# Moving two loads to later places in the block, and turning the inner order of a spreading copy

## Chip, cores and metric

The kernel runs on one core of one Trainium2 chip. The metric is device time in microseconds; the time before is the median of three runs.

## What is computed

```python
batch, n_heads, seq, head_dim = 8, 12, 1024, 64
# q, k: float32, (8, 12, 1024, 64)
out = np.einsum('bhid,bhjd->bhij', q, k)   # float32, (8, 12, 1024, 1024)
```

These are attention scores for 96 heads, without scaling or softmax. The inputs are 50.33 MB, the output is 402.65 MB.

## The kernel before

**Blocks, parts, pairs.** The first 8 heads are done by the class `First` in a start phase. The other 88 heads form 11 blocks ("units") of 8 heads. A block has two `Part`s (number 2u and 2u + 1), and a part has two passes `g` = 0 and 1. One pass computes two heads at once and is called a pair here; so a block has four pairs, and the 22 parts have 44.

**Loads.** `load(2u, ...)` brings Q of block u, `load(2u + 1, ...)` brings K, each 2048 KB, into a tile x_sb of `in_pool`, which has two buffers. A load can therefore be issued only when the tile of the block before last has been read by all its casts. ACT's queue issues these loads.

**Casts on POOL.** `Part.cast` turns a part's Q and K from float32 into float16 and stacks the heads on the partitions. It fills four `half_sb` tiles (Q in two pieces, then K in two), each by four casts of 32 partitions. `half_pool` has four buffers, so a cast into a tile waits until DVE has transposed what the tile held, a part earlier.

**Transposes on DVE (L208, L212).** `Part.transpose(x, c)` turns one half tile. For K it goes through `step_sb` and a copy that puts the elements in order.

**Spaced weights on DVE (L222).** `Part.space(g)` writes the turned Q of two heads into a tile that is zero otherwise (`spaced_even` for g = 0, `spaced_odd` for g = 1): head s = 0 lies on partitions 0 to 63 in the even columns, head s = 1 on partitions 64 to 127 in the odd columns. It is two copies of 64 partitions x 1024 elements. A 128 x 128 slice of the tile is then the weights of a product that yields 64 rows of each of the two heads.

**Products and copies (L75, L76).** `Part.scores(g, side)` makes 16 products of 128 x 1024 for a pair, each of two matmuls into a PSUM tile (four tiles), and copies each to the output tile `o_sb`: copies 1, 4, 7, 10 and 13 (counted from 0) by DVE, the others by ACT. Then SP issues one DMA of 8192 KB for the pair (L238). `out_pool` has two buffers, so a pair's first copies wait until the output of the pair before last has landed.

**The order is written by hand.** `pin` keeps each engine's instructions in program order. The dictionary `side` says what is emitted behind which copy. Behind copy 13 of g = 0 stand `space(1)` of the same part and three of the next part's four transposes; behind copy 13 of g = 1 stand the fourth transpose, `transpose(1, 1)`, and `space(0)` of the next part. Before the change the loads stood at these places: in the last pair of a block (odd part, g = 1) Q of the block after next behind copy 2 and K behind copy 12, both on ACT's queue. The casts of part n + 3 were emitted behind part n.

Of the kernel before, what the change touches and what calls it, by code (L numbers as in the profile page):

```python
# [13 lines left out]
def kernel(  # L14
# [6 lines left out]
    nc = tc.nc  # L21

    B, H, S, D = q.shape
    NT = S // P
# [19 lines left out]
    spaced = [spaced_even, spaced_odd]  # L44
# [46 lines left out]
    class First:  # L91
# [7 lines left out]
        def load(self):  # L99
            m = S * D // P  # L100
            for n in range(self.N if self.N == 2 else 1):
                for x in range(2):
                    start = (self.first + n) * S
                    count = S if self.N == 2 else self.N * S
                    src = (qf, kf)[x][start : start + count]
                    width = count * D // P
                    pin(
                        (nc.sync, nc.scalar)[x].dma_start(
                            out=self.raw[x][:, n * m : n * m + width],
                            in_=src.rearrange("(p r) d -> p (r d)", p=P),  # L110
                        )
                    )
# [66 lines left out]
    class Part:  # L179
# [35 lines left out]
                )  # L215

        def space(self, g):
            sp = spaced[g].rearrange("c t (i a) s -> c a t i s", a=4)
            for s in range(2):
                cs = slice(s * D, (s + 1) * D)  # L220
                qT = self.turned[0][cs].rearrange("c (a t g i) -> c g a t i", a=4, t=2 * NT, g=2)
                pin(nc.vector.tensor_copy(out=sp[cs, :, :, :, s], in_=qT[:, g]))  # L222

        def scores(self, g, side):
# [48 lines left out]
    def do_for(number, name, *args):  # L273
        if number < len(parts):
            getattr(parts[number], name)(*args)
# [18 lines left out]
    for n in range(4):  # L294
        side = {1: [lambda n=n: do_for(0, "transpose", *divmod(n, 2))]}
# [5 lines left out]
    for number, part in enumerate(parts):  # L301
        for g in range(2):
            side = {13: []}
            if g:
                side[13].append(lambda: do_for(number + 1, "transpose", 1, 1))
                side[13].append(lambda: do_for(number + 1, "space", 0))
            else:
                side[13].append(lambda: part.space(1))
                for x, c in ((0, 0), (0, 1), (1, 0)):
                    side[13].append(lambda x=x, c=c: do_for(number + 1, "transpose", x, c))  # L310
            if number == g == 0:
                side[2] = [lambda: load(3, nc.scalar)]
            if number % 2 and g:
                unit = number // 2
                side[2] = [lambda: load(2 * (unit + 2), nc.scalar)]
                side[12] = [lambda: load(2 * (unit + 2) + 1, nc.scalar)]
            part.scores(g, side)
        if number == 0:
            do_for(2, "cast")
        do_for(number + 3, "cast")  # L320


# [28 lines left out]
```

## Time and profile before

| | |
|---|---|
| median of three runs | 1082.76 us (1079.37 to 1083.43) |
| profiled execution, time | 1080.31 us |
| profiled execution, span | 1078.5 us |
| granted TensorE clock, mean | 0.72 |
| DVE, PE, ACT, POOL busy | 65%, 50%, 47%, 47% |
| DMA traffic | 420 GB/s over the span |

The engines are PE (matmul), PEld (its weight loads), DVE, ACT, POOL and SP; a q behind the name means the engine's sequencer, which issues DMAs. A row of a group of instructions reads: line, engine, operation, output <- input, shapes, count | busy us, mean ns | idle time ahead of them and what ended it. A row of the timeline begins with the start and the duration in us; brackets hold the idle time before it and what ended that. A row of a window gives the length, each engine's busy time (number of instructions), the granted TensorE clock, the DMA engines' busy share and GB/s. A row of a DMA queue gives packets, MB and the share of the time of all 16 DMA engines.

### The profile page before, as it was taken

What the parts mean: (1) busy time and instruction counts of PE and PEld (TensorE: products, weight loads), DVE (VectorE), ACT (ScalarE), POOL (GpSimd) and SP (SyncE); (2) the same over time, 40 slices, a digit from 0 to 9 for tenths busy, and PEclk for the clock granted to TensorE, in tenths of its full rate; (3) what the DMA queues carried; (4) which work ended last, traced back from release to release, by engine and by line L of the source; (5) the groups of instructions that cost most, each with busy time, mean ns of one, the idle gap of its engine ahead of it and who ended that gap; (6) DMA issues with size and microseconds to landing.
All of it is one profiled execution on the core that took longest, in us unless ns stands there. A gap on an engine that the chain in (4) does not pass through costs nothing.

```text
span 1078.5 us, 4965 instructions
## 1 busy us (share of the span) xinstructions
PE 542.9 (50%) x1568; PEld 188.9 (18%) x1568; DVE 706.4 (65%) x451; ACT 511.6 (47%) x546; POOL 510.4 (47%) x384
## 2 busy tenths in 40 slices
PE   6963454455454445444545454544454545464550
PEld 3321121111111111111111111211111111121210
DVE  3835667675677667768567765776856776578640
ACT  5963454344453445534446344553444634464550
POOL 6971743646437354354643636435464363643000
PEclk9997667676686766767678666876667866687775
DMA  9999999999999999999899999999999999999998
GB/s 378 430 430 430 443 430 414 429 428 380 439 428 427 390 429 432 394 448 430 370 444 436 420 400 426 428 391 434 445 377 448 436 420 399 426 430 428 443 442 360
DMA packets 12122, 453.30 MB, mean 420 GB/s; under 512 B 1344, under 2 KB 1344, under 8 KB 2368
## 3 DMA queue, kind: packets, MB, share of 16 engines
q1 hardware_dynamic: 8352, 406.85, 87.3%
q10 hardware_dynamic: 3744, 46.14, 11.3%
q8 instruction: 12, 0.20, 0.1%
q14 instruction: 14, 0.11, 0.0%
HBM read 50.33 MB, written 402.65 MB: 420 GB/s over the span
## 4 chain that ended last, share of the span: by engine, by line
DMA 48%; PE 17%; DVE 14%; ACT 10%; POOL 5%; issue 2%; ACTq 0%; SPq 0%; DVEq 0%
DMA out_dram<-o_sb 42%; PE ps L75 17%; ACT o_sb L76 10%; DVE spaced_even L222 6%; POOL half_sb L85 5%; DMA out_dram<-early 3%; DMA out_dram<-singles 2%; DVE o_sb L76 2%; DVE spaced_odd L222 2%; DVE step_sb L208 2%; DVE kT L212 1%; DVE qT L208 0%; DMA early<-in_q_dram 0%; PE ps L131 0%; ACT singles L76 0%
## 5 line engine op out<-in xcount | busy, mean ns | idle before, releaser
L85 POOL CAST half_sb<-x_sb 32x1024 f16<-32x1024 f32 x352 | 484.9, 1378 | 460.7 <-DVE qT L208 338.0
L76 ACT COPY o_sb<-ps 128x1024 f32<-128x1024 f32 x484 | 453.5, 1041 | 519.0 <-DMA out_dram<-o_sb 326.6
L76 DVE COPY o_sb<-ps 128x1024 f32<-128x1024 f32 x220 | 269.4, 1224 | 317.1 <-PE ps L75 197.4
L75 PE MATMUL ps<-kT,spaced_odd 128*128 128x512 f16 x704 | 257.1, 530 | 265.8 <-ACT o_sb L76 135.6
L75 PE MATMUL ps<-kT,spaced_even 128*128 128x512 f16 x704 | 225.9, 476 | 224.2 <-DVE spaced_even L222 185.9
L75 PEld LDWEIGHTS <-spaced_odd 128*128 128x128 f16 x704 | 87.2, 127 | 435.7 <-issue 293.4
L75 PEld LDWEIGHTS <-spaced_even 128*128 128x128 f16 x704 | 79.8, 116 | 370.5 <-DVE spaced_even L222 196.2
L222 DVE COPY spaced_even<-qT 64x1024 f16<-64x1024 f16 x44 | 140.2, 3187 | 0.3
L222 DVE COPY spaced_odd<-qT 64x1024 f16<-64x1024 f16 x44 | 107.0, 2431 | 1.0
L212 DVE COPY kT<-step_sb 128x1024 f16<-128x1024 f16 x44 | 62.5, 1420 | 1.6
L75 PE MATMUL ps<-kT,qT 64*128 64x512 f16 x128 | 56.0, 613 | 9.0 <-ACT early L76 6.3
L208 DVE STREAM_TRANSPOSE step_sb<-half_sb 128x1024 f16<-128x1024 f16 x44 | 53.7, 1220 | 3.9 <-POOL half_sb L85 3.9
L208 DVE STREAM_TRANSPOSE qT<-half_sb 128x1024 f16<-128x1024 f16 x44 | 52.3, 1227 | 0.7
L76 ACT COPY early<-ps 128x1024 f32<-128x1024 f32 x32 | 30.0, 1150 | 8.5 <-POOL half_sb L85 6.3
L76 ACT COPY singles<-ps 128x1024 f32<-128x1024 f32 x28 | 26.5, 1190 | 4.2 <-PE ps L75 4.2
L75 PEld LDWEIGHTS <-qT 64*128 64x128 f16 x128 | 18.7, 154 | 44.4 <-issue 42.1
L85 POOL CAST half_sb<-early 32x1024 f16<-32x1024 f32 x16 | 16.5, 1033 | 4.4 <-DMA early<-in_q_dram 3.7
L143 DVE STREAM_TRANSPOSE kT<-half_sb 128x1024 f16<-128x1024 f16 x2 | 9.8, 4908 | 0.0
L143 DVE STREAM_TRANSPOSE qT<-half_sb 128x1024 f16<-128x1024 f16 x2 | 9.6, 4793 | 0.0
L133 DVE COPY qT<-ps 128x1024 f16<-128x1024 f16 x2 | 2.4, 1224 | 9.6 <-PE ps L131 9.6
L76 DVE COPY singles<-ps 128x1024 f32<-128x1024 f32 x4 | 4.9, 1224 | 4.3 <-PE ps L75 4.3
L131 PE MATMUL ps<-ident,half_sb 128*128 128x128 f16 x32 | 4.1, 310 | 5.9 <-POOL half_sb L120 5.8
(13 smaller groups left out, 15.8 us busy)
## 6 DMA issues: line engine op xcount, KB each, us to landing
x_sb<-in_k_dram ACTq DMA_DIRECT2D x11, 2048.0 KB, 13.3
x_sb<-in_q_dram ACTq DMA_DIRECT2D x10, 2048.0 KB, 19.4
out_dram<-singles SPq DMA_DIRECT2D x4, 4096.0 KB, 22.9
out_dram<-early SPq DMA_DIRECT2D x4, 4096.0 KB, 26.3
x_sb<-in_q_dram SPq DMA_DIRECT2D x1, 2048.0 KB, 19.6
early<-in_k_dram ACTq DMA_DIRECT2D x4, 256.0 KB, 5.5
early<-in_q_dram SPq DMA_DIRECT2D x4, 256.0 KB, 5.0
early<-in_q_dram SPq DMA_DIRECT2D x1, 1024.0 KB, 10.3
```

The lines of the kernel that those rows point to most:

```text
L75: pin(nc.tensor.matmul(ps[:, at], weights, kT[:, at]))
L76: pin(copy(out=dst, in_=ps))
L85: nc.gpsimd.tensor_copy(out=half_sb[to : to + QUAD].rearrange("p (r d) -> p r d", d=32), in_=raw[b : b + QUAD, rows, h],)
L131: pin(nc.tensor.transpose(t_ps[:, t], self.halves[x][:, t], ident))
L133: pin(copy(out=dst, in_=t_ps.rearrange("c t m -> c m t")))
L143: nc.vector.transpose(out=dst.rearrange("c (i r) -> c r i", i=QUAD), in_=self.halves[x, part].rearrange("p (r i) -> p r i", i=QUAD),)
L208: pin(nc.vector.transpose(out=dst.rearrange("c (r i) -> c r i", i=QUAD), in_=src))
L212: nc.vector.tensor_copy(out=kT[:, c], in_=step_sb.rearrange("c (r i) -> c i r", i=QUAD))
L222: pin(nc.vector.tensor_copy(out=sp[cs, :, :, :, s], in_=qT[:, g]))
```

## The change

The access patterns of `space` are turned: the innermost dimension of both sides is now `a` (4 elements: 4 bytes apart in the spaced tile, 1024 bytes apart in the turned Q) where it was `i` (16 elements: 16 bytes apart in the spaced tile, side by side in the turned Q). The same elements go to the same places.

The load of Q is emitted behind copy 14 (the 15th) of the block's last pair, and that of K behind copy 8 (the 9th) of the next block's first pair. The casts of the two parts that come next but one are emitted together behind each even part, so that they stand behind both loads.

```diff
         def space(self, g):
-            sp = spaced[g].rearrange("c t (i a) s -> c a t i s", a=4)
+            sp = spaced[g].rearrange("c t (i a) s -> c t i a s", a=4)
             for s in range(2):
                 cs = slice(s * D, (s + 1) * D)
-                qT = self.turned[0][cs].rearrange("c (a t g i) -> c g a t i", a=4, t=2 * NT, g=2)
+                qT = self.turned[0][cs].rearrange("c (a t g i) -> c g t i a", a=4, t=2 * NT, g=2)
                 pin(nc.vector.tensor_copy(out=sp[cs, :, :, :, s], in_=qT[:, g]))
...
-            if number == g == 0:
-                side[2] = [lambda: load(3, nc.scalar)]
-            if number % 2 and g:
-                unit = number // 2
-                side[2] = [lambda: load(2 * (unit + 2), nc.scalar)]
-                side[12] = [lambda: load(2 * (unit + 2) + 1, nc.scalar)]
+            if number % 2 == g:
+                side[14 if g else 8] = [lambda: load(number + 3, nc.scalar)]
             part.scores(g, side)
-        if number == 0:
-            do_for(2, "cast")
-        do_for(number + 3, "cast")
+        if number % 2 == 0:
+            do_for(number + 2, "cast")
+            do_for(number + 3, "cast")
```

## Prediction

> **What bounds the kernel now.** I read the page first (span, traffic, the chain of waits), then the list of waits, then the windows, then the timeline of one block engine by engine.
>
> ```profile
> span 1078.5 us, 4965 instructions
> PE 542.9 (50%) x1568; PEld 188.9 (18%) x1568; DVE 706.4 (65%) x451; ACT 511.6 (47%) x546; POOL 510.4 (47%) x384
> HBM read 50.33 MB, written 402.65 MB: 420 GB/s over the span
> DMA 48%; PE 17%; DVE 14%; ACT 10%; POOL 5%; issue 2%; ACTq 0%; SPq 0%; DVEq 0%
> ```
>
> No engine is busy over 65%, and DMA is the largest part of the chain that ended last. The question is whether the DMA engines are ever short of work. Three windows answer it; the last two columns are the DMA share and GB/s.
>
> ```profile
> 160.00:970.00 810.00, 399.53 (x1162) 138.06 (x1160) 559.46 (x362) 373.34 (x399) 400.74 (x288) 0.70 0.99 420
> 970.00:1065.00 95.00, 42.69 (x128) 14.92 (x128) 54.52 (x37) 43.44 (x47) 10.02 (x5) 0.69 1.00 431
> 531.00:541.00 10.00, 7.19 (x20) 2.59 (x21) 4.45 (x4) 6.37 (x7) 3.18 (x2) 0.58 0.82 287
> ```
>
> In the last block, which has no loads, the traffic runs at 431 GB/s; in the nine blocks with loads at 420; and inside one of those there are 10 us at 287. So the DMA engines are the limit nearly always, and there is a hole once a block. The list of waits names what makes the hole (total us, times, longest):
>
> ```profile
> ACT o_sb L76 <- DMA out_dram<-o_sb: 326.6, 30, 15.5
> ...
> ACT o_sb L76 <- POOL half_sb L85: 127.2, 17, 11.4
> ```
>
> The 326.6 us are harmless: ACT waits for an output buffer, so DMA is behind. The 127.2 us are not: nothing in ACT's copies reads half_sb. What does wait for POOL are the loads that ACT issues, because their x_sb tile is free only after POOL's casts. ACT's timeline around the block change at 511 us:
>
> ```profile
> 511.27 1.93 ACT L76 COPY o_sb<-ps 128x1024 f32<-128x1024 f32 x2 [8.68 <-DMA out_dram<-o_sb]
> 516.40 0.33 ACTq L177 DMA_DIRECT2D x_sb<-in_q_dram  x1
> 516.78 6.51 ACT L76 COPY o_sb<-ps 128x1024 f32<-128x1024 f32 x7 [3.59 <-POOL half_sb L85]
> 534.26 0.34 ACTq L177 DMA_DIRECT2D x_sb<-in_k_dram  x1
> 534.63 12.10 ACT L76 COPY o_sb<-ps 128x1024 f32<-128x1024 f32 x13 [11.34 <-POOL half_sb L85]
> 562.12 4.89 ACT L76 COPY o_sb<-ps 128x1024 f32<-128x1024 f32 x5 [15.38 <-DMA out_dram<-o_sb]
> ...
> 582.41 10.18 ACT L76 COPY o_sb<-ps 128x1024 f32<-128x1024 f32 x11 [9.60 <-DMA out_dram<-o_sb]
> 601.71 1.93 ACT L76 COPY o_sb<-ps 128x1024 f32<-128x1024 f32 x2 [9.12 <-DMA out_dram<-o_sb]
> ```
>
> The pair that starts at 511.27 is the last of its block. Its Q load stops ACT for 3.59 us and its K load for 11.34 us, because the K load needs a cast that needs a transpose which stands behind the 14th copy of this very pair. POOL and DVE show that loop, and SP shows its price:
>
> ```profile
> 507.08 13.62 POOL L85 CAST half_sb<-x_sb 32x1024 f16<-32x1024 f32 x12 [15.28 <-DVE qT L208]
> 524.89 9.33 POOL L85 CAST half_sb<-x_sb 32x1024 f16<-32x1024 f32 x4 [4.19 <-DVE step_sb L208]
> ```
>
> ```profile
> 523.59 1.23 DVE L208 STREAM_TRANSPOSE step_sb<-half_sb 128x1024 f16<-128x1024 f16 x1
> ...
> 525.79 6.46 DVE L222 COPY spaced_even<-qT 64x1024 f16<-64x1024 f16 x2
> ```
>
> ```profile
> 536.59 0.54 SPq L238 DMA_DIRECT2D out_dram<-o_sb  x1
> ```
>
> Transpose at 523.59, casts until 534.22 (four take 9.33 us beside the spaced copies of 525.79, where twelve took 13.62), K load at 534.26, last ACT copies, output issued at 536.59. That is 25.3 us after the pair got its buffer at 511.27, where an undisturbed pair takes 10.2 us (ACT's row at 582.41: 10.18). Over 25 us after the last landing the output before it must have left, and SP's queue is empty: this is the hole of the 287 GB/s row.
>
> **How big the hole is.** An output is 128 x 16 x 1024 x 4 bytes, 8192 KB. Between the buffer waits that end at 582.41 and 601.71 one output passes with no load beside it: 19.30 us. A load is 8 heads x 1024 x 64 x 4 bytes, 2048 KB, a quarter. The Q load issued at 606.39, alone:
>
> ```profile
> 606.39 0.33 ACTq L177 DMA_DIRECT2D x_sb<-in_q_dram  x1
> ```
>
> ```profile
> DMA to landing us min/median/max: 19.4/19.4/19.4
> ```
>
> It lands at 625.8. From 582.4 to 625.8 two outputs and this load pass, 2.25 outputs in 43.4 us, and 2.25 x 19.30 is 43.4: a load between queued outputs costs its bytes and no more. A block (four outputs, Q, K) is 4.5 x 19.30 = 86.9 us of full DMA. Measured:
>
> ```profile
> 221.70 2.84 ACT L76 COPY o_sb<-ps 128x1024 f32<-128x1024 f32 x3 [8.96 <-PE ps L75]
> ```
>
> ```profile
> 942.07 2.84 ACT L76 COPY o_sb<-ps 128x1024 f32<-128x1024 f32 x3 [9.10 <-DMA out_dram<-o_sb]
> ```
>
> These are the same point of the block, eight blocks apart: 720.4 / 8 = 90.05 us. The hole is 3.2 us a block, nine times (the loads of the third to the eleventh block are issued at this place): 28.8 us at most. The other bound prices a load by its queue's row of the whole page:
>
> ```profile
> q1 hardware_dynamic: 8352, 406.85, 87.3%
> q10 hardware_dynamic: 3744, 46.14, 11.3%
> ```
>
> That is 2.31 us of all engines per MB of q1 (nearly all outputs) and 2.64 for q10 (loads), so the two loads of a block, 4.19 MB, would take 1.4 us more and the hole would be 1.8 us. I hold to 3.2, because the 43.4 us are a stretch in which DMA had no gap, and q10's row contains the gaps.
>
> **The change, part by part.**
>
> Q load, from behind copy 3 to behind copy 15 of the last pair. It needs the first 8 of the 12 casts at 507.08, over at 516.4. Copy 15 of an undisturbed pair is done some 9.2 us after the buffer, at about 520.5: no wait, 4 us to spare. The 3.59 us stall goes. Behind it on ACT stands one copy; the issue costs 0.33 us, as before.
>
> K load, from behind copy 13 of that pair to behind copy 9 of the next block's first pair. With no stall the 14th copy is over near 520.4, the transpose follows, and the four casts end by 531 even at their present 9.33 us. The next pair gets its buffer when the output in flight has landed, near 533, and its ninth copy is some 6 us later, 539: no wait, 8 us to spare. The 11.34 us stall goes, and the output now issued at 536.59 goes out near 522, while the one before it is still in flight for over 10 us. The hole is closed from both sides.
>
> What comes later: the loads land later, and share the engines with outputs all the time. How fast is a load then? While both queues had work (520 to 531 us; packets, MB, share):
>
> ```profile
> q1 hardware_dynamic: 57, 3.21, 67.4%
> q10 hardware_dynamic: 70, 1.15, 24.3%
> ```
>
> 1.15 MB of load in 11 us, so 2.10 MB take 20 us. Q: issued 520.5, landed near 543, where the first pair's transposes (behind its copy 14, near 542) let POOL start on it: level, at most a few us late. K follows on the same queue and lands near 563. It is first needed for the transpose behind copy 14 of the block's third pair: that pair gets its buffer two outputs and a load after 533, near 579, and reaches copy 14 near 588. The four casts between take up to 9.3 us: 16 us to spare. SP's queue holds only outputs and is not touched. The casts are written out later, but POOL's order of parts is the same: nothing. In the first block the K load goes from behind copy 3 to behind copy 9, once, and its data is used a pair later: nothing.
>
> The spaced copies (L222). Before, 16 elements are read side by side and written 16 bytes apart; now four are read 1024 bytes apart and written 4 bytes apart. The rows of this copy and its neighbours:
>
> ```profile
> L222 DVE COPY spaced_even<-qT 64x1024 f16<-64x1024 f16 x44 | 140.2, 3187 | 0.3
> L222 DVE COPY spaced_odd<-qT 64x1024 f16<-64x1024 f16 x44 | 107.0, 2431 | 1.0
> L212 DVE COPY kT<-step_sb 128x1024 f16<-128x1024 f16 x44 | 62.5, 1420 | 1.6
> ...
> L143 DVE STREAM_TRANSPOSE kT<-half_sb 128x1024 f16<-128x1024 f16 x2 | 9.8, 4908 | 0.0
> ```
>
> L212 reads 64 bytes apart and writes densely: 1.42 us. L143 writes 64 bytes apart: 4.91 us. So far-apart writes are dear and far-apart reads cheap. I bound the new copy by 1.4 and 4.9 us and take 1.4, the row with the like reads, no row having reads as far apart as 1024 bytes. It saves 8 x (2.81 - 1.4) = 11 us of DVE per block, and I count it at nothing: what hides it is the wait for output buffers. If that cover were gone, it would be a gain.
>
> The Trainium skill (SBUF — State Buffer, the note on cachelines under Door 1: The DMA port swizzle) says that an SBUF line has 16 bytes, that full rate needs two or more hits on a line, and that every access to a new line pays. By it the writes come right (four on a line) and the reads go wrong (each on a new line), which is the rule behind rival C below. The L212 row, with such reads at 1.42 us, bears it out only in small part, and C has its chance by that.
>
> **Sum.** 28.8 us is the whole hole. I take 2.9 of the 3.2 us per block, leaving 0.3 for handovers between outputs: 26 us. Span 1078.5 - 26 = 1052.5; the profiled execution took 1080.31, 1.8 more than its span, so 1054.3; that execution was 2.45 under the median of 1082.76, so 1056.5 for a median.
>
> **Rivals.**
>
> *A: part of the hole stays.* The loads land 20 us after they start, and Q is only level with its first use. If POOL's casts slip far enough that one pair in four still sends its output late, half the gain stays away: 1082.8 - 13 = 1069.8. For it: Q's landing. Against: what waits for POOL comes a pair and a half later.
>
> *B: no change.* Loads beside queued outputs would cost more than their bytes, and what ACT gains the DMA loses: 1082. The 43.4 us against 43.4 above speak against it; only for K's part there is no such row.
>
> *C: slower, by the far reads.* DVE's chain per pair is not far under DMA's time:
>
> ```profile
> 545.00 4.87 DVE L222 COPY spaced_odd<-qT 64x1024 f16<-64x1024 f16 x2
> ...
> 562.14 1.22 DVE L76 COPY o_sb<-ps 128x1024 f32<-128x1024 f32 x1 [6.87 <-DMA out_dram<-o_sb]
> ...
> 570.97 1.23 DVE L208 STREAM_TRANSPOSE step_sb<-half_sb 128x1024 f16<-128x1024 f16 x1
> ...
> 590.85 4.88 DVE L222 COPY spaced_odd<-qT 64x1024 f16<-64x1024 f16 x2
> ```
>
> ```profile
> 579.69 3.59 PE L75 MATMUL ps<-kT,spaced_even 128*128 128x512 f16 x8 [8.98 <-DVE spaced_even L222]
> ```
>
> From 545.00 to 570.97, less the 6.87 us wait, are 19.1 us; from 570.97 to 590.85, less some 2.0 us (a first product from 579.69 is ready near 580.4, its buffer at 582.41), 17.9. Twice both is 74 us a block, with eight spaced copies of 2.81 us mean in it, 22.5. DVE reaches the 86.9 us when a copy takes (86.9 - 74 + 22.5) / 8 = 4.4 us, and the 90.05 us at 4.8. At L143's 4.9 us a block is 90.7; nine blocks are 6 us worse than now, and the last one, now 4 x 19.30 = 77.2, becomes 90.7, 13 more: about 1102. It decides from 4.8 us per copy on, twice the undisturbed row.
>
> **How the numbers follow.** About 0.5% (5.4 us) is what a measurement of this kernel can tell from no change. Forecast 0.78, rival A 0.09, rival B 0.05, rival C 0.08. Faster takes the forecast and A: 0.87; same 0.05; slower 0.08. The forecast's own range is 1051 (28.8 us off, and the 2.45 us not added: 1051.5) to 1066 (the hole of 1.8 us, nine times, off 1082.76: 1066.6); reaching to A I give 1051 to 1070.
>
> **What would show it.** Right: ACT's wait for POOL's half_sb in the loop near 0 from 127.2; loads issued without a wait; windows of loaded blocks at 430 GB/s; same points of the block 87 us apart; landing of Q near 20 us; the L222 rows at 1 to 2 us with no effect of their own. Wrong: a block still at 90 us with 430 GB/s absent; DVE or PE waiting for POOL casts; L222 above 4.4 us, with ACT no longer waiting for out_dram.

## The result and the profile after

The changed kernel takes 1077.19 us in the median of 20 runs (1072.29 to 1081.84), the kernel before 1082.36 in 20 runs beside it (1079.37 to 1083.55). The runs after scatter more than those before. The ratio is 0.9953, with a 95% interval of 0.9939 to 0.9967; ratios here and below leave out one execution, the longest of run 9, which is marked as slow. The forecast was 1056.5, the range 1051 to 1070: the sign came, and a fifth of the size (5.2 us of 26). The profiled execution after took 1076.11 us, with a span of 1074.3.

The page after, in its parts on engines, DMA queues and the chain of waits:

```profile
span 1074.3 us, 4965 instructions
PE 540.6 (50%) x1568; PEld 190.6 (18%) x1568; DVE 579.9 (54%) x451; ACT 515.3 (48%) x546; POOL 429.4 (40%) x384
...
q1 hardware_dynamic: 8352, 406.85, 88.4%
q10 hardware_dynamic: 3744, 46.14, 10.5%
...
DMA 69%; ACT 13%; PE 8%; POOL 4%; issue 2%; ACTq 0%; POOLq 0%
```

DMA's part of the chain rose from 48 to 69%, and DVE, which had 14%, is gone from it. The engines no longer hold the DMA up, and yet the traffic of the loaded blocks is short of the 430 GB/s that was expected of them (the first row is nine blocks with loads, the second the last block; the last two columns are DMA share and GB/s):

```profile
160.00:970.00 810.00, 393.32 (x1152) 138.15 (x1152) 454.62 (x364) 375.95 (x398) 331.32 (x290) 0.70 1.00 424
970.00:1065.00 95.00, 43.51 (x128) 15.33 (x128) 40.61 (x34) 41.36 (x44) 3.85 (x3) 0.68 1.00 430
```

The share is 1.00 where it was 0.99, and still a block with loads moves only 424 GB/s: the DMA engines are busy, and not at their best. The two queue rows say the same for the whole span. (A packet is the piece of a transfer that one DMA engine moves at a time; here 64 KB of an output, 16 KB of a load.) Before, the packets of both queues took 98.6% of 1078.5 us, 1063 us, and 15 us were left; after, they take 98.9% of 1074.3, again 1062 us, with 12 left. So the change removed some 3 us of idle time and made the same bytes hardly cheaper. Within this sum it did move time: q10, nearly all of it loads, falls from 11.3% of 1078.5 to 10.5% of 1074.3, 9 us less, and q1, the outputs, rises from 87.3% to 88.4%, 8 us more. The loads became cheaper, and the outputs dearer by almost as much.

ACT's timeline at the place that the prediction read (the four pairs of one block and the first of the next):

```profile
508.00 4.89 ACT L76 COPY o_sb<-ps 128x1024 f32<-128x1024 f32 x5 [8.29 <-DMA out_dram<-o_sb]
...
516.84 0.33 ACTq L177 DMA_DIRECT2D x_sb<-in_q_dram  x1
...
530.95 5.81 ACT L76 COPY o_sb<-ps 128x1024 f32<-128x1024 f32 x6 [11.84 <-DMA out_dram<-o_sb]
535.80 0.33 ACTq L177 DMA_DIRECT2D x_sb<-in_k_dram  x1
...
557.12 4.89 ACT L76 COPY o_sb<-ps 128x1024 f32<-128x1024 f32 x5 [14.78 <-DMA out_dram<-o_sb]
...
579.53 4.89 ACT L76 COPY o_sb<-ps 128x1024 f32<-128x1024 f32 x5 [11.47 <-DMA out_dram<-o_sb]
...
598.84 8.73 ACT L76 COPY o_sb<-ps 128x1024 f32<-128x1024 f32 x9 [8.18 <-DMA out_dram<-o_sb]
```

SP's timeline at the same place:

```profile
519.14 0.54 SPq L238 DMA_DIRECT2D out_dram<-o_sb  x1
```

The stalls of 3.59 and 11.34 us are gone: both loads are issued without a wait, and the last pair's output leaves at 519.14, 11.1 us after its buffer came at 508.00, where it was 25.3 us. The next buffer comes only at 530.95, so SP's queue does not run dry here. But the intervals between buffers are 22.95, 26.17, 22.41 and 19.31 us. The last carries no load. Four of it are 77.2, the block is 90.8: the two loads cost 13.6 us, where their bytes, two quarters of 19.31, are 9.7. (This is one block, longer than the mean; the mean, 89.78, stands with run 10.)

The landing times (last number, median us) show the same:

```profile
x_sb<-in_k_dram ACTq DMA_DIRECT2D x11, 2048.0 KB, 36.1
x_sb<-in_q_dram ACTq DMA_DIRECT2D x10, 2048.0 KB, 29.6
```

They were 13.3 for K (issued into the hole) and 19.4 for Q. And the spaced copies:

```profile
L222 DVE COPY spaced_even<-qT 64x1024 f16<-64x1024 f16 x44 | 69.4, 1578 | 0.3
L222 DVE COPY spaced_odd<-qT 64x1024 f16<-64x1024 f16 x44 | 56.6, 1287 | 1.0
```

They halved, from 3.19 and 2.43 us to 1.58 and 1.29, and DVE's busy time went from 706 to 580 us.

### The profile page after: what moved, and what is told of

Its sections match the earlier page's. It is cut to its first block, busy times and chain, and to the rows that moved or that the text cites. A ratio compares the mean times of both kernels' runs of the same rounds, so it can differ in the third digit from the quotient of the medians.

```text
span 1074.3 us, 4965 instructions
## 1 busy us (share of the span) xinstructions
PE 540.6 (50%) x1568; PEld 190.6 (18%) x1568; DVE 579.9 (54%) x451; ACT 515.3 (48%) x546; POOL 429.4 (40%) x384
## 3 DMA queue, kind: packets, MB, share of 16 engines
q1 hardware_dynamic: 8352, 406.85, 88.4%
q10 hardware_dynamic: 3744, 46.14, 10.5%
## 4 chain that ended last, share of the span: by engine, by line
DMA 69%; ACT 13%; PE 8%; POOL 4%; issue 2%; ACTq 0%; POOLq 0%
DMA out_dram<-o_sb 64%; ACT o_sb L76 13%; PE ps L75 8%; POOL half_sb L85 4%; DMA out_dram<-early 3%; DMA early<-in_q_dram 1%; ACT early L76 1%; ACTq L177 0%; POOL spaced_even L269 0%; POOL spaced_odd L269 0%; ACTq L76 0%; ACTq L342 0%; POOLq L85 0%
## 5 line engine op out<-in xcount | busy, mean ns | idle before, releaser
L85 POOL CAST half_sb<-x_sb 32x1024 f16<-32x1024 f32 x352 | 403.9, 1148 | 535.1 <-DMA x_sb<-in_q_dram 192.2
L75 PE MATMUL ps<-kT,spaced_even 128*128 128x512 f16 x704 | 248.6, 518 | 257.4 <-ACT o_sb L76 121.4
L75 PE MATMUL ps<-kT,spaced_odd 128*128 128x512 f16 x704 | 232.1, 493 | 233.8 <-ACT o_sb L76 181.3
L75 PEld LDWEIGHTS <-spaced_even 128*128 128x128 f16 x704 | 86.2, 125 | 420.1 <-issue 266.6
L75 PEld LDWEIGHTS <-spaced_odd 128*128 128x128 f16 x704 | 82.6, 120 | 383.3 <-issue 290.3
L222 DVE COPY spaced_even<-qT 64x1024 f16<-64x1024 f16 x44 | 69.4, 1578 | 0.3
L212 DVE COPY kT<-step_sb 128x1024 f16<-128x1024 f16 x44 | 57.1, 1298 | 1.6
L222 DVE COPY spaced_odd<-qT 64x1024 f16<-64x1024 f16 x44 | 56.6, 1287 | 1.0
L85 POOL CAST half_sb<-early 32x1024 f16<-32x1024 f32 x16 | 16.6, 1036 | 4.5 <-DMA early<-in_q_dram 3.8
L133 DVE COPY qT<-ps 128x1024 f16<-128x1024 f16 x2 | 2.4, 1224 | 10.3 <-PE ps L131 10.3
## 6 DMA issues: line engine op xcount, KB each, us to landing
x_sb<-in_k_dram ACTq DMA_DIRECT2D x11, 2048.0 KB, 36.1
x_sb<-in_q_dram ACTq DMA_DIRECT2D x10, 2048.0 KB, 29.6
out_dram<-early SPq DMA_DIRECT2D x4, 4096.0 KB, 25.3
```

What stands on the lines that cost most here:

```text
L75: pin(nc.tensor.matmul(ps[:, at], weights, kT[:, at]))
L85: nc.gpsimd.tensor_copy(out=half_sb[to : to + QUAD].rearrange("p (r d) -> p r d", d=32), in_=raw[b : b + QUAD, rows, h],)
L133: pin(copy(out=dst, in_=t_ps.rearrange("c t m -> c m t")))
L212: nc.vector.tensor_copy(out=kT[:, c], in_=step_sb.rearrange("c (r i) -> c i r", i=QUAD))
```

## The experiments

All are edits of the changed kernel, unless it says of the kernel before. Four groups of them ran, each beside the kernel before, whose median was 1081.72, 1081.16, 1081.59 and 1082.04 us.

The theories at the start. **Theory 1:** with the hole gone the 16 DMA engines drift apart, and a buffer is free only when the last of them has landed its share. **Theory 2:** a load that starts beside queued outputs makes packets slow. **Theory 3:** the loads' move brought nothing; the small gain is that of the shorter spaced copies.

**1. The moved loads alone** (the old patterns in `space`).

```diff
-            sp = spaced[g].rearrange("c t (i a) s -> c t i a s", a=4)
+            sp = spaced[g].rearrange("c t (i a) s -> c a t i s", a=4)
...
-                qT = self.turned[0][cs].rearrange("c (a t g i) -> c g t i a", a=4, t=2 * NT, g=2)
+                qT = self.turned[0][cs].rearrange("c (a t g i) -> c g a t i", a=4, t=2 * NT, g=2)
```

> The change without its new spaced copies: only the two loads (and the emission of the casts) are moved. Theory 1 (the 16 DMA engines drift apart once the hole of each block change is gone, and a buffer is free only when the last engine has landed) and theory 2 (a load that starts beside queued outputs makes packets slow) both put the limit in the DMA, so DVE's longer copies stay covered: 1077, within 3 us of the whole change. Theory 3 (the small gain came from the shorter spaced copies, the moved loads brought nothing): 1082.

Measured: 1077.19 us (ratio 0.995, 0.9929 to 0.9972), the time of the whole change. Theory 3 falls: the moved loads bring the gain by themselves.

**2. The spaced copies alone** (the kernel before with the new patterns of `space`; the diff is that of the change, reversed for everything but `space`).

> The change without the moved loads: only the new order inside the spaced copies. In the profile after, the four casts beside the spaced copies take 6.58 us instead of 9.33, so the K load and the output behind it go out some 2.7 us earlier, while the stall that brings the engines into step stays. Theory 1: the hole shrinks from 3.2 to about 1 us and the engines stay in step, 1065 to 1072, so faster than the whole change. Theory 2: the K load still runs alone at the block change, 1072 to 1078. Theory 3: 1077, the whole gain of the change.

Measured: 1073.14 us (ratio 0.9913, 0.989 to 0.9937), better than the whole change. Its POOL and ACT timelines show what this half, which the prediction had counted at nothing, does:

```profile
520.19 6.57 POOL L85 CAST half_sb<-x_sb 32x1024 f16<-32x1024 f32 x4 [5.06 <-DVE step_sb L208]
```

```profile
508.39 1.93 ACT L76 COPY o_sb<-ps 128x1024 f32<-128x1024 f32 x2 [9.06 <-DMA out_dram<-o_sb]
...
511.20 2.85 ACT L76 COPY o_sb<-ps 128x1024 f32<-128x1024 f32 x3 [0.88 <-POOL half_sb L85]
...
527.16 1.93 ACT L76 COPY o_sb<-ps 128x1024 f32<-128x1024 f32 x2 [8.43 <-POOL half_sb L85]
```

The four casts that the K load waits for take 6.57 us instead of 9.33, beside copies that are now shorter; ACT's stalls shrink from 3.59 to 0.88 and from 11.34 to 8.43. Both halves work on the same hole, which is a reason for them not to add. More than that: on top of the short copies, moving the loads makes it worse, 1073.1 to 1077.2 (the ratios' intervals, up to 0.9937 here and from 0.9939 for the whole change, just part).

**3. The loads on SP's queue.**

```diff
-                side[14 if g else 8] = [lambda: load(number + 3, nc.scalar)]
+                side[14 if g else 8] = [lambda: load(number + 3, nc.sync)]
```

> The changed kernel with the loads inside the loop issued on SP's queue instead of ACT's, so that loads and outputs stand in one queue, in order, and never take turns. Theory 2: the slow packets go and a block falls from 89.7 to about 87.5 us, 1055 to 1062. Theory 1: the engines drift all the same, 1072 to 1080.

Measured: 1066.95 us (ratio 0.9853, 0.983 to 0.9876). The same loads, in the queue of the outputs, gain 10 us over the change.

**4. Outputs of half the size** (each pair's output leaves in two DMAs of 4096 KB, out of four buffers; the loads as in the change).

```diff
-    out_pool = ctx.enter_context(tc.tile_pool(name="out_pool", bufs=2))
+    out_pool = ctx.enter_context(tc.tile_pool(name="out_pool", bufs=4))
...
-            o_sb = out_pool.tile([P, 2 * NT, S], F32, tag="out")
...
+            for h in range(2):
+                o_sb = out_pool.tile([P, NT, S], F32, tag="out")
...
+                        out=heads[2 * self.part + g, h],
```

> The changed kernel with each pair's output in two halves, in four output buffers of half the size (same memory), each half with a DMA of its own. The first half goes out 8 copies earlier and a buffer is free after half the data. Theory 1: engines that are ahead find the next output waiting and are no longer starved, 1055 to 1068. Theory 2: the loads meet the outputs as before, 1074 to 1080.

Measured: 1069.62 us (ratio 0.9879, 0.9854 to 0.9904): most of that gain too, with two queues.

```profile
q1 hardware_dynamic: 14688, 406.85, 89.0%
```

The page counts 14688 packets for the outputs' queue instead of 8352, for the same 406.85 MB, so the packets are smaller as well (32 KB), and the loads land in 20 us. The run therefore does not tell the wait for the last engine from the packets' turns.

**5. No loads** (the loads of the blocks from the third on are left out, and the casts read the tiles of the second again).

```diff
     def load(number, queue):
...
+        if unit >= 2:
+            raws[unit, x] = raws[1, x]
+            return
```

> The changed kernel without the loads of the third to the eleventh block (their parts are computed from the second block's tiles, so the output of those heads is not the reference's). 18 loads of 2048 KB are 4.83 us each at the rate of outputs, 87 us. Theory 2 (loads make packets slow, some 1.6 us a block): 1077 - 87 - 14 = 976, and every pair 19.3 us apart. Theory 1 (the engines drift by themselves and starve): 985 to 990, with the spread of the completions growing as it does now.

Measured: 976.97 us. This prices a load: 18 of them are left out, so one costs (1077.2 - 977.0) / 18 = 5.57 us in the change. It also shows outputs with nothing beside them:

```profile
425.54 4.89 ACT L76 COPY o_sb<-ps 128x1024 f32<-128x1024 f32 x5 [9.20 <-DMA out_dram<-o_sb]
...
445.14 10.39 ACT L76 COPY o_sb<-ps 128x1024 f32<-128x1024 f32 x11 [8.80 <-DMA out_dram<-o_sb]
464.73 4.89 ACT L76 COPY o_sb<-ps 128x1024 f32<-128x1024 f32 x5 [9.19 <-DMA out_dram<-o_sb]
...
484.35 10.42 ACT L76 COPY o_sb<-ps 128x1024 f32<-128x1024 f32 x11 [8.48 <-DMA out_dram<-o_sb]
503.91 4.89 ACT L76 COPY o_sb<-ps 128x1024 f32<-128x1024 f32 x5 [9.14 <-DMA out_dram<-o_sb]
```

Every interval is 19.6 us, 78.37 for four, so outputs among themselves leave no gap that grows, as theory 1 alone would have it; it takes a load. But the unit is not the prediction's 19.30, and that was no slip of reading: in the last block of the change, which has no loads either, ACT's waits end 19.3 us apart:

```profile
976.76 4.68 ACT L76 COPY o_sb<-ps 128x1024 f32<-128x1024 f32 x5 [8.86 <-DMA out_dram<-o_sb]
...
996.08 4.89 ACT L76 COPY o_sb<-ps 128x1024 f32<-128x1024 f32 x5 [8.88 <-DMA out_dram<-o_sb]
...
1015.39 10.51 ACT L76 COPY o_sb<-ps 128x1024 f32<-128x1024 f32 x11 [8.19 <-DMA out_dram<-o_sb]
1034.69 4.89 ACT L76 COPY o_sb<-ps 128x1024 f32<-128x1024 f32 x5 [8.80 <-DMA out_dram<-o_sb]
```

The landing records, which have 16 shares for each output, tell the two apart. In the first blocks of run 5 nine in ten shares (each output's in order of landing) come 19.3 us after the share of the same rank of the output before, but the last share 19.57 to 19.61, and a buffer is free only with the last. In the last blocks of the kernel before and of the change, too, four of seven outputs have a share that takes 19.5 to 19.7, but it is not the last of its output. So I count an output at 19.6 us over many blocks, in which the slow share has time to become the last. That it is the same DMA engine each time is likely and not shown: the records name no engine.

**6. Half outputs and SP's queue together** (the edits of 3 and 4).

> Half-size outputs in four buffers and the loads on SP's queue, both at once. If the two runs before gained by different means (no taking turns; no starving), the gains add: 1077 - 10 - 7.5 = 1060. If both gained by the same thing, that an engine that is ahead always finds something in its queue: 1064 to 1067, no better than the better of the two.

Measured: 1069.66 us (ratio 0.9893, 0.9869 to 0.9917). The two gains don't add. That they are one and the same is not shown by it; the packet times below speak against it.

**7. Both loads behind a 9th copy**, Q in the next block's first pair and K in its second, on ACT's queue: is it the start of a load just ahead of an output's issue that costs (theory 2a), or the start of any load beside outputs (2b)?

```diff
-            if number % 2 == g:
-                side[14 if g else 8] = [lambda: load(number + 3, nc.scalar)]
+            if number == g == 0:
+                side[8] = [lambda: load(3, nc.scalar)]
+            if number and number % 2 == 0:
+                side[8] = [lambda: load(number + 2 + g, nc.scalar)]
```

> The changed kernel with both loads later: Q behind the 9th copy of the next block's first pair, K behind the 9th copy of its second. In the profile after, the Q load goes out 2.3 us ahead of an output's DMA and slow packets follow (1 to 1.7 us a block), the K load 6.6 us ahead of one and few follow (0.1 to 0.4). Theory 2a (a load just ahead of an output's issue is what makes packets slow): 1062 to 1070. Theory 2b (any load's start does it): 1074 to 1080. If K now comes too late for its casts, POOL and DVE wait and it is slower than 1080.

Measured: 1083.94 us (ratio 1.0027, 1.0015 to 1.0039). POOL's wait for Q rose from 192 to 284 us, so the casts are later too, and the run is not a pure test; but the gain that 2a promised is not there.

**8. Only the K load moved** (the kernel before; K behind the 9th copy of the next block's first pair, Q and `space` as before).

```diff
+            if number % 2 == g == 0:
+                side[8] = [lambda: load(number + 3, nc.scalar)]
             if number % 2 and g:
                 unit = number // 2
                 side[2] = [lambda: load(2 * (unit + 2), nc.scalar)]
-                side[12] = [lambda: load(2 * (unit + 2) + 1, nc.scalar)]
```

> The kernel before with the K load alone moved (behind the 9th copy of the next block's first pair, casts emitted as in the change); Q stays behind the 3rd copy of the last pair, spaced copies old. The 11 us stall goes, the 3.6 us stall stays; the output of the block's last pair goes out some 14 us earlier and the Q load 12 us ahead of it. Theory 2a: no slow packets, 1060 to 1068. Theory 2b and theory 1: 1074 to 1080, like the whole change.

Measured: 1079.6 us (ratio 0.9984, 0.9971 to 0.9997). ACT's waits for POOL's half_sb fall from 127.2 to 31.1 us in all, and 1.6 us come of it. With Q started well ahead of the output's issue the loads are no cheaper, and output packets are slow as often as in the change (328 of 64 KB over 2.5 us, there 327): 2a falls.

**9 and 10. Earlier on ACT's queue; later on SP's.** Run 3 differs from the change in two things: it has one queue, and its loads are issued earlier. Theory 4a: the time at which a load is issued decides. Theory 4b: the single queue decides, because the DMA engines no longer take turns between two.

```diff
-                side[14 if g else 8] = [lambda: load(number + 3, nc.scalar)]
+                side[4 if g else 0] = [lambda: load(number + 3, nc.scalar)]
```

> The run with the loads on SP's queue also sent them earlier: in its profile Q 2.6 us and K 17.3 us after the last pair got its buffer, where the change has 8.9 and 27.9. Here the changed kernel keeps ACT's queue and sends them earlier: Q behind the 5th copy of the last pair, K behind the first copy of the next block's first pair. Theory 4a (it was the earlier time): 1064 to 1070. Theory 4b (it was the single queue, in which loads and outputs do not take turns): 1074 to 1080.

```diff
-            if number % 2 == g:
-                side[14 if g else 8] = [lambda: load(number + 3, nc.scalar)]
+            if number == g == 0:
+                side[8] = [lambda: load(3, nc.sync)]
+            if number and number % 2 == g == 0:
+                side[0] = [lambda: load(number + 2, nc.sync)]
+                side[8] = [lambda: load(number + 3, nc.sync)]
```

> The other half of that test: SP's queue, but late. Both loads are emitted in the next block's first pair, so in the one queue they stand behind the last pair's output, Q some 11 us and K some 19 us after that pair got its buffer, and both land after it, near 50 and 55 us. Theory 4b (single queue): 1064 to 1070, as with the early loads there. Theory 4a (earlier time): 1077 or slower; the casts would wait for the loads longer than in the change.

Measured: 1092.8 us earlier on ACT's queue (1081.98 to 1100.83; ratio 1.0084, 1.005 to 1.0118), 1067.13 later on SP's (0.9864, 0.9848 to 0.9881). The time of issue doesn't decide and the queue does: 4b stands, 4a falls. That the early loads lose so much was not expected. The profiled execution (1084.18 us, one of the shorter) has still more slow output packets and more idle time than the change, as the table below has it; no run here says why. In run 10 ACT's timeline reads:

```profile
436.12 10.40 ACT L76 COPY o_sb<-ps 128x1024 f32<-128x1024 f32 x11 [8.73 <-DMA out_dram<-o_sb]
455.70 4.89 ACT L76 COPY o_sb<-ps 128x1024 f32<-128x1024 f32 x5 [9.18 <-DMA out_dram<-o_sb]
...
485.06 4.89 ACT L76 COPY o_sb<-ps 128x1024 f32<-128x1024 f32 x5 [18.15 <-DMA out_dram<-o_sb]
...
505.23 4.89 ACT L76 COPY o_sb<-ps 128x1024 f32<-128x1024 f32 x5 [9.43 <-DMA out_dram<-o_sb]
...
524.83 10.42 ACT L76 COPY o_sb<-ps 128x1024 f32<-128x1024 f32 x11 [8.71 <-DMA out_dram<-o_sb]
```

Here both loads lie in one interval of 29.36 us, between two outputs: 9.76 us more than 19.60, or 4.88 each, a quarter of an output. That is a load at its bytes, but the next interval, 20.17 us, is longer too, so the two cost 10.3 in this block. Over eight blocks, from the same point to the same point of ACT's timeline, run 10 and then the change:

```profile
239.48 4.89 ACT L76 COPY o_sb<-ps 128x1024 f32<-128x1024 f32 x5 [8.24 <-DMA out_dram<-o_sb]
...
948.45 1.93 ACT L76 COPY o_sb<-ps 128x1024 f32<-128x1024 f32 x2 [8.90 <-DMA out_dram<-o_sb]
```

```profile
239.17 4.89 ACT L76 COPY o_sb<-ps 128x1024 f32<-128x1024 f32 x5 [8.68 <-DMA out_dram<-o_sb]
...
957.42 2.84 ACT L76 COPY o_sb<-ps 128x1024 f32<-128x1024 f32 x3 [8.19 <-DMA out_dram<-o_sb]
```

A block takes 708.97 / 8 = 88.62 us in run 10 and 718.25 / 8 = 89.78 in the change; nine times the difference is 10.4 us, about what lies between the two medians (10.1). (The two profiled spans differ by less, 7.7 us: outside these eight blocks the change is the shorter one by 1.5.) The rows of run 10's window and of its queues:

```profile
160.00:960.00 800.00, 384.85 (x1152) 135.84 (x1152) 465.49 (x363) 373.83 (x398) 344.86 (x289) 0.72 1.00 429
```

```profile
span 1066.6 us, 4965 instructions
...
q1 hardware_dynamic: 11088, 446.70, 97.7%
q10 hardware_dynamic: 1008, 6.29, 1.5%
```

The loaded blocks now move 429 GB/s, as the prediction had expected of the change. The packets take 99.2% of 1066.6, 1058 us, and 8.5 us are left. Against the page after (1062.5 and 11.8) the larger part of the 7.7 us between the spans lies in faster packets, the rest in less idling.

**11. Run 10 with the old patterns of `space`** (the edit of 1 on top).

> The run with late loads on SP's queue, but with the old spaced copies (3.2 and 2.4 us instead of 1.8 and 1.3). The spaced copies alone gained 8.6 us in the kernel before. If they gained only by making the K load's stall of ACT shorter, they are worth nothing where no load waits on ACT: 1067, as with the new copies. If DVE's time is short in itself: 1072 to 1076.

Measured: 1067.28 us (ratio 0.9863, 0.9846 to 0.9879). Its spaced copies are back at 3.17 and 2.43 us, at no cost. Where no load waits on ACT, the short copies are worth nothing, as the prediction had it (run 1 says the same of the change); in run 2, where loads do wait, they are worth 8.6 us.

**12. K on SP's queue, Q on ACT's**, at the places of the change.

```diff
-                side[14 if g else 8] = [lambda: load(number + 3, nc.scalar)]
+                side[14 if g else 8] = [lambda: load(number + 3, nc.scalar if g else nc.sync)]
```

> The changed kernel with the K load alone on SP's queue; Q stays on ACT's queue behind the 15th copy. Theory 4b (loads and outputs that take turns from two queues lose time, each load its part): halfway between the change and the single queue, 1070 to 1074. If one of the two loads does all the harm: 1067 (it is K) or 1077 (it is Q).

Measured: 1070.35 us (ratio 0.9894, 0.9874 to 0.9913). Of the 10.2 us between the change and run 3, K's queue gives 6.8 and Q's the rest.

**Packet times side by side.** The trace has a start, a duration, a queue and a size for every packet. The sums, divided by the 16 DMA engines, in us; small packets (12 to 13 us in each run) are left out, and idle is the span less all packets:

| run | span | outputs | loads | idle | output packets of 64 KB over 2.5 us, of 5632 |
|---|---|---|---|---|---|
| before | 1078.5 | 930.0 | 122.0 | 14.0 | 30 |
| the change | 1074.3 | 938.9 | 112.3 | 10.5 | 327 |
| 2, spaced copies alone | 1073.2 | 930.5 | 121.4 | 8.7 | 56 |
| 3, SP's queue | 1066.0 | 932.2 | 114.4 | 7.2 | 83 |
| 4, half outputs | 1067.5 | 938.7 | 108.6 | 7.2 | all are of 32 KB |
| 5, no loads | 975.3 | 931.5 | 20.5 | 11.0 | 31 |
| 9, earlier on ACT's queue | 1082.4 | 945.7 | 109.3 | 14.9 | 522 |
| 10, later on SP's queue | 1066.6 | 932.1 | 114.3 | 8.0 | 68 |

Against the kernel before, the change saves 10 us of load packets and 3.5 of idle time, and pays 9 in output packets. Run 2 gains by idle time alone. Run 3 takes 7 of the 9 us back, and 3 of idle time, and pays 2 in loads. Run 4 gains by loads and idle time and leaves the outputs dear, so its gain is not that of run 3.

The records also show the turns. Between 200 and 960 us, 2005 output packets start among the 2112 load packets of the change, nearly one for one, and 617 among the 2048 of run 3 and 402 among the 2056 of run 10, where most load packets follow each other. (Among: between the first and the last load packet of a group that no pause over 3 us divides.)

**The best version** is the change with both loads on SP's queue: 1066.95 us (run 3) or 1067.13 (run 10), 1.4 to 1.5% under the kernel before and 0.9% under the change.

## Why the prediction was right and wrong

**The hole's cause: right; its size as idle time: wrong.** The loads are issued without a wait, ACT's row for half_sb in the list of waits (127.2 us before) has no counterpart in the loop, and the output goes out 11.1 us after its buffer. But all idle time of the kernel before is 14.0 us, not 28.8, and the change took away 3.5 of it.

**The chain's slack: right.** No step of the transposes or products came to wait for a late cast in a way that moves the end: DMA's share of the chain grew, and the intervals end with landings. Rival A asked for late casts; the casts do start later, but it is not they that hold the outputs. (For the third pair's buffer, two outputs and a load after 533, the sum gives 576 and not the 579 that I wrote; the trace has 579.53, with the loads dearer than I thought.)

**The spaced copies: size right, worth wrong.** I took 1.4 us and they are 1.58 and 1.29, so rival C, which began at 4.8, never came near. The trace agrees with the row of L212: far reads cheap, far writes dear. The slowing of far reads, for which C had drawn on the Trainium skill's note on cachelines (SBUF — State Buffer, Door 1: The DMA port swizzle), is not seen. "I count it at nothing" failed as a statement on the kernel before: run 2 gains 8.6 us by it, through the casts beside which the copies run. It held where I used it, behind loads that no longer wait (runs 1 and 11).

**"A load between queued outputs costs its bytes and no more": the step that failed.** It rested on one stretch of 43.4 us with one Q load, and the reading of that stretch is right; but no output was queued behind that load (SP issued the next at 626.46, after the landing at 625.8), so it was not the case that the change makes. In the change a load costs 5.57 us (by its bytes, a quarter of 19.6, 4.90), in run 10, with the places changed again but the queue shared, (1067.1 - 977.0) / 18 = 5.01. This is rival B's mechanism, which I gave 0.05: what ACT gained, the DMA largely lost, 9 us of it in slower output packets. It was no rival to be dismissed by one coincidence of sums, as the landing times of the change show (36.1 and 29.6 us instead of the 20 that I took from an 11 us window).

**"86.9 us of full DMA a block": too low, as far as the runs show.** With 19.6 for an output (run 5) a block is 4.5 x 19.6 = 88.2 us; run 10's 88.62 leave 0.4 for handovers, where I had 0.3, so the form of the sum holds and its unit was off: 19.30 is what an output takes while the slow share is not the last. The measured 90.05 then contain 1.85 us to be had, not 3.2; nine times that is 16.6. That is nearly my other bound, from the queue rows (1.8 us), which I had put aside; it came near by luck, for it made the loads dear and not the outputs. Put on the median, 1082.4 - 16.6 = 1065.8: runs 3 and 10 came within 1.4 us of it.

So the 28.8 us at which I put the hole divide so: some 12 were not there by the unit of run 5, about 10 are lost to the second queue, 5.2 came, and a rest of 1.2 us may be the handovers. The forecast's own sum has a slip besides: 1054.3 + 2.45 is 1056.8, not 1056.5. It changes nothing.

**What stays open.** That two queues cost is shown (runs 1, 3, 9, 10, 11, 12), and so is where the cost lies: in more slow output packets and more idle time. Why the packets become slow is not shown. The Trainium skill (DMA: Bandwidth & Descriptors, Queues, rings and completion order) has each DMA engine go round its queues packet by packet, which would stretch a load over more of an output, and smaller output packets (run 4) less so. The trace agrees: load and output packets stand nearly one for one in the change, and a load lands in 30 to 36 us there and in 20 in run 4. Whether it is these turns that slow the output packets, or that inputs and outputs move at the same time, no run here separates. The 16 shares of one output land up to 9.5 us apart in the change, where it was 0.6 to 2.7 before. But runs 3 and 10 also come to 6 to 7 us between the shares and run 5 to 8 without any loads, so theory 1's drift doesn't explain what the change loses; its price is the step from 19.3 to 19.6 us.

## What to carry to other kernels

Where outputs keep the DMA engines full, try the loads in the same queue as the outputs, at a place where nothing holds them up: here the queue was worth twice what taking the stall out of ACT had brought. A unit cost read between two buffer waits should be read again where nothing else runs (run 5), since a buffer waits for the last of 16 shares and the last may not yet be the slow one. The queue rows' total of packet time leaves the idle time as its rest, and closing a hole can give back no more than that; a packet's own time can change as well, for the worse in the change and back again in run 3. Two edits that work on one hole should be costed each against the kernel with the other in place.

## What the hardware showed that I had not expected

- The queue matters, not only the bytes: with places changed as well, 2048 KB cost 5.57 us from ACT's queue beside outputs of SP's queue, and 5.01 from SP's own. The Trainium skill (DMA: Bandwidth & Descriptors, "Issuing engines are not separate DMA queues") says that transfers interleave on the same 16 engines whoever issues them, and that issuing from several only saves issue time. The interleaving agrees with the packet records; but here the choice of queue was not neutral, it cost 10 us (run 3 against the change).
- The 16 shares of one output land up to 9.5 us apart, and one of them is slow: in the first blocks of run 5 nine in ten follow each other in 19.3 us and the last in 19.6, and the buffer waits for it.
- An output packet of 64 KB takes 2.42 us; in the change 327 of 5632 take over 2.5 us, in the kernel before 30, in run 10, with one queue, 68.
- A copy of 64 x 1024 elements of 2 bytes takes 1.29 us when its writes are 4 bytes apart and its reads 1024, and 2.43 us when its writes are 16 apart and its reads side by side.
